# Index queries for 384 of 512 tokens, reordered layer beginnings, and chunk decays read by small DMAs

## The chip, the cores and the metric

The kernel runs on one core of a Trainium2 chip. The metric is device time in microseconds (us), the median of the runs. An execution takes 1.7 us more than its span in the profile, which runs from the first to the last instruction of the core.

## The reference

Two layers act on 512 tokens of width 1024. Each layer projects its input once and feeds two branches: an attention branch that keeps, for every query, the 128 keys with the best score of a small "indexer", and a gated linear attention (GLA) that is scanned in chunks of 64 tokens. A gated convolutional feed-forward part follows.

```python
# indexer and attention, per block of 128 queries
dots = einsum('bqhd,bsd->bqhs', q_idx, k_idx) * IDX_DIM ** -0.5
score = einsum('bqhs,bqh->bqs', relu(dots), w_idx * IDX_HEADS ** -0.5)
score = where(admissible, score, -inf)          # chunk-causal, chunks of 64
top_val, top_idx = lax.top_k(score, topk)       # topk = 128
...
# GLA, per chunk of 64
cum = cumsum(lac, axis=1); total = cum[:, -1]
k_dec = kc * exp(total[:, None] - cum)
state = exp(total)[..., None] * state + einsum('bchk,bchv->bhkv', k_dec, vc)
out = einsum('bchk,bhkv->bchv', qc, state)
```

The first 128 queries have at most 128 admissible keys, so that every one of them is kept.

## The kernel before

All projections run on TensorE as three matmuls per 128x128 block of weights (`mm3`, lines 149 to 153), since every operand is split into a high and a low half. Weights come in tiles of 512 KB by SP's queue (`pump`); ScalarE (ACT) writes the high half (line 145) and VectorE (DVE) the low half (line 146). Results of the projections are split in the same way by the same two lines. `fm_chunk` gives four banks of 128 features by 512 tokens, `tm_chunk` four banks of 128 tokens by 512 features; the next chunk uses these four banks again, so its first matmul on a bank waits for the evacuation of the one before.

A layer is a list of projections in a fixed order: index queries (iq), a small chunk (index keys, gate ranks), GLA queries (gq0 to gq3), keys (gk) and values (gv0, gv1), then queries, keys and values of the attention (aq, ak, av). In layer 0 iq comes first; in layer 1 iq is computed in two halves of 256 tokens, since the norm that ends layer 0 delivers its tokens late. Everything else is a task: a generator that `tick()` advances by one step after every six matmuls of the projections. These are the rotation tables, the index keys, the decays (`decay_task`), the loads (`load_task`), the index scores with top-k (`index_task`), the scans of GLA and then the attention. A framework turns the whole into one fixed order of instructions per engine, and gives evacuations and weight splits priority.

`staged` evacuates iq, aq and ak: bank 0 is rotated on DVE (lines 504 to 507), banks 1 to 3 are only split, and all are written to DRAM by POOL's queue (line 498) and read back per pair of heads by `load_task` (lines 525, 529, 530), since two halves of a head meet only there. `index_task` runs top-k as 16 rounds per block of 128 queries, for blocks of 512, 384 and 256 keys: a round finds the eight largest (MAX8, line 578) and takes them out (MATCH_VALUE_LOAD and MATCH_REPLACE8, line 579), each waiting for the one before.

`decay_task` multiplies the log decays with a triangle of ones (`tri`, line 449) for the suffix sums of each chunk and with two columns (`ends`, line 451) for the totals. ACT takes the exponentials; the totals are transposed (line 460) and become `dec`, which the scans multiply their state with. The evacuation of gk multiplies with the exponentials and waits for the whole task.

Of the kernel before, what the change touches and what calls it, by code (L numbers as in the profile page):

```python
# [56 lines left out]
class Trunk:  # L57
# [91 lines left out]
    def mm3(self, out, lh, ll, rh, rl, start, stop):  # L149
        mm = self.nc.tensor.matmul  # L150
        mm(out, lh, rl, start=start, stop=False)  # L151
        mm(out, ll, rh, start=False, stop=False)  # L152
        mm(out, lh, rh, start=False, stop=stop)  # L153
# [13 lines left out]
    def tm_chunk(self, l, chunk, evac):  # L167
        ps = [self.bank(self.acc) for _ in range(TB)]
        for g in range(4):
            w = self.weight((l, chunk, g)).rearrange("p z (k n) -> p z k n", k=2)  # L170
            for tb in range(TB):
                c = slice(tb * 128, (tb + 1) * 128)
                for kk in range(2):
                    k = 2 * g + kk
                    self.mm3(ps[tb], self.xT[:, k, 0, c], self.xT[:, k, 1, c], w[:, 0, kk], w[:, 1, kk],
                             k == 0, k == KT - 1)
# [5 lines left out]
    def fm_chunk(self, l, chunk, evac, toks=((0, S),), between=None, k_outer=False):  # L182

        ws = []
        ps = [self.bank(self.acc) for _ in range(4)]
        for n, (t0, t1) in enumerate(toks):
            if n:
                between()
            for g in range(4):
                if not n:  # L190
                    ws.append(self.weight((l, chunk, g)))
                w = ws[g].rearrange("p z (k n) -> p z k n", k=2)

                def mm(m, kk):
                    k, c = 2 * g + kk, slice(m * 128, (m + 1) * 128)
                    self.mm3(ps[m][:, t0:t1], w[:, 0, kk, c], w[:, 1, kk, c], self.xT[:, k, 0, t0:t1],
                             self.xT[:, k, 1, t0:t1], k == 0, k == KT - 1)
                if k_outer:
                    for m in range(4):
                        mm(m, 0)  # L200
                for m in range(4):
                    for kk in range(k_outer, 2):
                        mm(m, kk)
                    if len(toks) == 1 or m % 2:
                        self.tick()
                    if g == 3 and t1 == S:
                        with self.tc.high_priority():
                            evac(m, ps[m])
# [9 lines left out]
    def constants(self):  # L218
        nc = self.nc
        c = self.cst  # L220
        self.ident = c.tile([128, 128], F32, name="ident")
        make_identity(nc, self.ident)
        trif = self.h()
        nc.gpsimd.memset(trif[:, :128], 1.0 / 16)
        nc.gpsimd.affine_select(trif[:, :128], trif[:, :128], pattern=[[-1, 128]], base=-1, channel_multiplier=1,
                                compare_op=ALU.is_ge, fill=0.0)
        nc.gpsimd.memset(trif[64:128, 0:64], 0.0)
        nc.gpsimd.memset(trif[:, 128:262], 0.0)
        nc.gpsimd.memset(trif[0:64, 134:135], 1.0 / 16)
        nc.gpsimd.memset(trif[64:128, 135:136], 1.0 / 16)  # L230
        self.tri = c.tile([128, 128], F32R, name="tri")
        nc.vector.tensor_copy(self.tri, trif[:, :128])
        self.ends = c.tile([128, 134], F32R, name="ends")
        nc.vector.tensor_copy(self.ends, trif[:, 128:262])
# [114 lines left out]
    def plan_all(self, l):  # L349
# [4 lines left out]
        for g in range(4):  # L354
            P((l, "iq", g), (a["w_tm"][l, TM_CHUNKS.index("iq"), g], None))
        small()
        for c in self.order:
            if c.startswith("gq"):
# [32 lines left out]
    order = ["gq0", "gq1", "gk", "gv0", "gq2", "gq3", "gv1", "aq", "ak", "av"]  # L391
# [19 lines left out]
    def decay_task(self):  # L411

        nc = self.nc
# [14 lines left out]
        tot = self.bank(self.tps)  # L428
        self.expE = [self.u(F32) for _ in range(2)]

# [10 lines left out]
        for _ in range(7):  # L441
            yield
        for tb in range(TB):
            lt = ahead
            if tb < TB - 1:
                ahead = parts(tb + 1)
            e = self.bank(self.sps)
            for z in (1, 0):
                nc.tensor.matmul(e, self.tri, lt[:, z], start=z == 1, stop=z == 0)
            for z in (1, 0):  # L450
                nc.tensor.matmul(tot, self.ends[:, 6 - 2 * tb:134 - 2 * tb], lt[:, z], start=tb == 0 and z == 1,
                                 stop=tb == TB - 1 and z == 0)
            last = self.after(last, act, self.expE[tb // 2][:, tb % 2], e, AF.Exp)
            yield
            yield
        t = self.h()
        nc.scalar.copy(t[:32], tot[:32])
# [3 lines left out]
        act(self.dec, ps[:, :GH * 32].rearrange("p (h c) -> p h c", h=GH)[:, :, :8], AF.Exp)  # L461
        yield

    def ik_task(self):

        nc = self.nc
        ps = self.bank(self.tps)
# [20 lines left out]
    def staged(self, dr):  # L488
# [4 lines left out]
        rotated = []  # L493

        def write(m, src):
            t = self.u()
            self.split(t[:, 0], t[:, 1], src)
            nc.gpsimd.dma_start(rows[m], t.bitcast(F32))

        def evac(m, ps):  # L500
            if m == 0:
                self.finish(self.tables)
                x, y = self.h(), self.h()
                v.tensor_mul(x, ps, self.ropeT[:, 0])
                v.tensor_mul(y[:64], ps[64:], self.ropeT[64:, 1])
                v.tensor_mul(y[64:], ps[:64], self.ropeT[:64, 1])
                v.tensor_add(x, x, y)
                rotated.append(x)
            else:
                write(m, ps)  # L510
                if m == 1:
                    write(0, rotated[0])
        return evac

    def load_task(self, dr, dst, low=None):

        rows = dr.rearrange("(q h) n -> q h n", h=HEADS)
        load = self.nc.gpsimd.dma_start
        for _ in range(4):
            yield  # L520
        for hp in range(4):
            src = rows[:, 2 * hp:2 * hp + 2]
            t = self.u()
            if low is None:
                load(t.bitcast(F32), src)
# [312 lines left out]
    def mixer(self, l):  # L838
# [8 lines left out]
        nc.gpsimd.memset(self.gl[32:64].bitcast(F32), 0.0)  # L847
        if l == 0:
            self.tables = self.spawn(self.table_task())
            self.fm_chunk(l, "iq", self.staged(dr["iq"]), k_outer=True)  # L850
            self.do_small(l, self.sps)
        else:
            self.finish(*self.norms[:2])

            def between():
                self.finish(*self.norms)
                self.do_small(l, self.sps)
            self.fm_chunk(l, "iq", self.staged(dr["iq"]), ((0, 256), (256, 512)), between)
        iqt = self.spawn(self.load_task(dr["iq"], iqT))
        ikt = self.spawn(self.ik_task())  # L860
        dct = self.spawn(self.decay_task())
        idx = self.spawn(self.index_task(iqT, [ikt, iqt]), 1)
        self.attnT = {}
        for c in self.order:
            if c == "gk":
# [7 lines left out]
            elif c.startswith("gq"):  # L873
                h = int(c[2:])
                ps = self.fm_tile(self.weight((l, "fm", FM["gq"] + h)))
                t = self.u()
                nc.scalar.mul(t[:, 0], ps, DK ** -0.5)
                nc.vector.scalar_tensor_tensor(t[:, 1], ps, DK ** -0.5, t[:, 0].bitcast(F32), op0=ALU.mult,
                                               op1=ALU.subtract)
                self.gq[h] = t  # L880
            elif c.startswith("gv") or c == "av":
# [8 lines left out]
                self.tm_chunk(l, c, evac)  # L890
                if c != "av":
                    scans.append(self.spawn(self.scan_task(2 * int(c[2]))))
            else:
                self.fm_chunk(l, c, self.staged(dr[c]))
                self.spawn(self.load_task(dr[c], *((qT, self.ql) if c == "aq" else (kT,))))
        self.finish(*scans)
# [22 lines left out]
        self.closing(l, "wout", self.merged, 0, KT, lambda tb: self.norm_task(tb, g, b, (5, 5, 6, 11)[tb]))  # L919

# [67 lines left out]
    def ffn(self, l):  # L988
# [31 lines left out]
        self.closing(l, "wdB", gT, KA, NF, (lambda tb: self.norm_out(tb, g, b)) if l == L - 1 else lambda tb: self.norm_task(tb, g, b, (5, 5, 6, 5)[tb]))  # L1020
# [82 lines left out]
```

## Time and profile before

| | |
|---|---|
| median of 3 runs | 1770.44 us (1769.88 to 1777.11) |
| the profiled execution | 1772.71 us, span 1771.0 us |
| TensorE (PE) busy, of the span | 1746.9 us, 99% |
| weight loads (PEld) | 1429.8 us, 81% |
| VectorE (DVE) | 1129.3 us, 64% |
| ScalarE (ACT) | 717.1 us, 40% |
| GpSimd (POOL) | 70.3 us, 4% |
| DMA, mean | 111 GB/s |

PE is busy almost without a pause, so the time is the work on PE plus the few places where it waits. Matmuls overlap: a matmul of 512 columns lasts 0.39 us in a row of the profile, but the next one starts earlier, and the spacing from start to start is what it costs. The other engines matter where PE waits for them, and DVE's share of 64% is a mean over stages that differ much.

### The profile page before, as it was taken

The numbers are of one execution on the slowest core, as the hardware profiler recorded it, in microseconds if no ns is written. First come the engines' busy times: TensorE is split into PE (matmuls) and PEld (weight loads), VectorE is DVE, ScalarE is ACT, GpSimd is POOL, SyncE is SP. The second block draws the span as 40 slices with busy tenths as digits, with TensorE's granted clock in tenths as the row PEclk, the third lists the DMA queues.
The fourth block names the chain that finished last, engine by engine and source line by source line (L and its number), as shares of the span: only waits on it lengthen the run. The fifth ranks groups of instructions, "written<-read, shape, count | busy, mean of one in ns | idle before, by whom it ended". The sixth has DMA issues, their size and how long they took to land.

```text
span 1771.0 us, 21726 instructions
## 1 busy us (share of the span) xinstructions
PE 1746.9 (99%) x8312; PEld 1429.8 (81%) x8312; DVE 1129.3 (64%) x2099; ACT 717.1 (40%) x1088; POOL 70.3 (4%) x113
## 2 busy tenths in 40 slices
PE   8999999999999999999999999999999999999997
PEld 6788787888888888888787878878888888888886
DVE  6699868633476663356667997876335766633656
ACT  5644456522225442144245444664222344422430
POOL 1000300000000000000010003000000000000000
PEclk9999999999999999999999999999999999999999
DMA  7322751232423322333353229312334233222331
GB/s 239 127 76 72 213 181 60 72 107 95 167 72 108 96 96 94 95 95 97 122 177 119 72 72 267 126 48 84 107 107 166 73 107 96 95 95 94 96 107 48
DMA packets 65172, 196.65 MB, mean 111 GB/s; under 512 B 7238, under 2 KB 9542, under 8 KB 65068
## 3 DMA queue, kind: packets, MB, share of 16 engines
q1 hardware_dynamic: 51312, 152.91, 27.4%
q0 software_dynamic: 8320, 29.36, 5.3%
q10 hardware_dynamic: 5436, 12.98, 2.1%
q8 instruction: 65, 1.06, 0.2%
q14 instruction: 39, 0.32, 0.1%
HBM read 178.46 MB, written 16.78 MB: 110 GB/s over the span
## 4 chain that ended last, share of the span: by engine, by line
PE 77%; DVE 14%; DMA 3%; issue 2%; ACT 2%; POOL 1%; SPq 0%; DVEq 0%; POOLq 0%; ACTq 0%
PE ps L152 24%; PE ps L151 24%; PE ps L153 24%; DVE w L146 2%; DVE sc L579 2%; DVE m L578 1%; DVE u L146 1%; PE ps L697 1%; DVE u L800 1%; DVE h L616 1%; DMA u<-aq 1%; POOL rs L333 1%; DMA raw<-in_w_tm 1%; PE ps L707 1%; DVE xT L146 1%
## 5 line engine op out<-in xcount | busy, mean ns | idle before, releaser
L146 DVE TENSOR_TENSOR w<-raw,w 128x1024 fp32r<-128x1024 f32 (+2 forms) x287 | 349.8, 1219 | 482.4 <-ACT w L145 480.2
L151 PE MATMUL ps<-xT,w 128*128 128x512 f32 (+1 forms) x1456 | 553.7, 380 | 3.0 <-DVE xT L146 2.5
L153 PE MATMUL ps<-xT,w 128*128 128x512 f32 (+1 forms) x1456 | 551.2, 379 | 0.0
L152 PE MATMUL ps<-xT,w 128*128 128x512 f32 (+1 forms) x1456 | 550.8, 378 | 0.0
L145 ACT CAST w<-raw 128x1024 fp32r<-128x1024 f32 (+2 forms) x287 | 300.0, 1045 | 500.2 <-PE ps L153 446.4
L151 PEld LDWEIGHTS ps<-xT,w 128*128 128x128 f32 x1456 | 273.7, 188 | 56.0 <-ACT w L145 3.3
L153 PEld LDWEIGHTS ps<-xT,w 128*128 128x128 f32 x1456 | 273.5, 188 | 50.7
L152 PEld LDWEIGHTS ps<-xT,w 128*128 128x128 f32 x1456 | 273.6, 188 | 49.2 <-DVE w L146 0.2
L151 PE MATMUL ps<-w,u 128*128 128x512 f32 (+1 forms) x488 | 192.0, 393 | 0.0
L153 PE MATMUL ps<-w,u 128*128 128x512 f32 (+1 forms) x488 | 190.9, 391 | 0.0
L152 PE MATMUL ps<-w,u 128*128 128x512 f32 (+1 forms) x488 | 190.9, 391 | 0.0
L145 ACT CAST u<-h 128x512 fp32r<-128x512 f32 (+1 forms) x126 | 77.9, 619 | 219.7 <-DVE h L983 111.3
L146 DVE TENSOR_TENSOR u<-h,u 128x512 fp32r<-128x512 f32 (+1 forms) x126 | 86.3, 688 | 40.0 <-ACT u L145 39.6
L153 PEld LDWEIGHTS ps<-w,u 128*128 128x128 f32 x488 | 91.6, 188 | 21.6
L151 PEld LDWEIGHTS ps<-w,u 128*128 128x128 f32 x488 | 91.7, 188 | 21.4
L152 PEld LDWEIGHTS ps<-w,u 128*128 128x128 f32 x488 | 91.7, 188 | 20.7
L151 PE MATMUL ps<-w,xT 128*128 128x512 f32 x256 | 102.2, 399 | 0.2
L152 PE MATMUL ps<-w,xT 128*128 128x512 f32 x256 | 101.0, 395 | 0.0
L153 PE MATMUL ps<-w,xT 128*128 128x512 f32 x256 | 100.9, 395 | 0.0
L152 PE MATMUL ps<-u,w 128*128 128x512 f32 x192 | 76.0, 396 | 0.0
L151 PE MATMUL ps<-u,w 128*128 128x512 f32 x192 | 75.4, 393 | 0.0
L153 PE MATMUL ps<-u,w 128*128 128x512 f32 x192 | 74.6, 388 | 0.0
(221 smaller groups left out, 1903.4 us busy)
## 6 DMA issues: line engine op xcount, KB each, us to landing
raw<-in_w_fm SPq DMA_DIRECT2D x160, 512.0 KB, 3.6
raw<-in_w_tm SPq DMA_DIRECT2D x55, 512.0 KB, 3.6
raw<-in_w_down SPq DMA_DIRECT2D x44, 512.0 KB, 3.4
u<-aq POOLq DMA_DIRECT2D x32, 256.0 KB, 11.1
raw<-in_w_mix_out SPq DMA_DIRECT2D x16, 512.0 KB, 3.5
iq<-u POOLq DMA_DIRECT2D x8, 512.0 KB, 4.5
u<-iq POOLq DMA_DIRECT2D x8, 512.0 KB, 6.5
aq<-u POOLq DMA_DIRECT2D x8, 512.0 KB, 4.0
```

What stands on the lines that cost most here:

```text
L145: first = self.nc.scalar.copy(hi, src)
L146: self.nc.vector.tensor_sub(lo, src, hi.bitcast(F32))
L151: mm(out, lh, rl, start=start, stop=False)
L152: mm(out, ll, rh, start=False, stop=False)
L153: mm(out, lh, rh, start=False, stop=stop)
L333: self.nc.gpsimd.tensor_tensor(r, ve, self.nhalf[:, :n], ALU.pow)
L578: nc.vector.max(m8, sc)
L579: nc.vector.match_replace(sc, m8, sc, TAKEN)
L616: nc.vector.scalar_tensor_tensor(state[:, i], old[:, i], self.dec[:, h, c:c + 1], o[:, i], op0=ALU.mult, op1=ALU.add)
L697: nc.tensor.transpose(ps[:, qb * 128:(qb + 1) * 128], P[qb][:, sb * 128:(sb + 1) * 128], self.ident)
L707: mm(out[:64], v[:, :64], PT[sb][:, 1], start=False, stop=False)
L800: nc.vector.scalar_tensor_tensor(x[:, c], x[:, c], r, b[:, c], op0=ALU.mult, op1=ALU.add)
```

## The change

It does five things.

1. iq is computed, rotated, written and loaded for tokens 128 to 511 alone (`t0`, `cut`): 96 matmuls of 384 columns in each layer instead of 512. In layer 1 it is no longer in halves; the four gq tiles are (`gq_halves`).
2. The matmuls with `ends` are gone. `tri` gets its columns 63 and 127 filled, so that rows 63 and 127 of each exponential hold the total decay of a chunk. Small DMAs of POOL's queue read these rows into the tile that is transposed (line 450 of the changed kernel), and others overwrite them with ones (line 452).
3. The order becomes gv0, small, iq, gq0, gq1, gk, gq2, gq3, gv1, aq, ak, av in layer 0, and gq0 to gq3, small, iq, gk, gv0, gv1, aq, ak, av in layer 1. Tasks and scans are spawned accordingly. The first group of gv0 starts with products of high halves.
4. Bank 0 of aq is copied raw by ACT (`late`) and rotated later, in `load_task`.
5. The norm that ends layer 0 waits 11 ticks instead of 5 for its last block.

```diff
-    def mm3(self, out, lh, ll, rh, rl, start, stop):
+    def mm3(self, out, lh, ll, rh, rl, start, stop, high_first=False):
...
+    def fm_chunk(self, l, chunk, evac, t0=0):
...
+                    self.mm3(ps[m][:, t0:], w[:, 0, kk, c], w[:, 1, kk, c], self.xT[:, k, 0, t0:],
+                             self.xT[:, k, 1, t0:], k == 0, k == KT - 1)
...
+        nc.gpsimd.memset(trif[0:64, 63:64], 1.0 / 16)
+        nc.gpsimd.memset(trif[64:128, 127:128], 1.0 / 16)
...
-    order = ["gq0", "gq1", "gk", "gv0", "gq2", "gq3", "gv1", "aq", "ak", "av"]
+    order = [["gv0", "small", "iq", "gq0", "gq1", "gk", "gq2", "gq3", "gv1", "aq", "ak", "av"],
+             ["gq0", "gq1", "gq2", "gq3", "small", "iq", "gk", "gv0", "gv1", "aq", "ak", "av"]]
...
-            for z in (1, 0):
-                nc.tensor.matmul(tot, self.ends[:, 6 - 2 * tb:134 - 2 * tb], lt[:, z], start=tb == 0 and z == 1,
-                                 stop=tb == TB - 1 and z == 0)
-            last = self.after(last, act, self.expE[tb // 2][:, tb % 2], e, AF.Exp)
...
+            last = self.after(last, act, E[:, tb % 2], e, AF.Exp)
+            nc.gpsimd.dma_start(t[2 * tb:2 * tb + 2], E[63:128:64, tb % 2])
+            if tb % 2:
+                nc.gpsimd.dma_start(E[63:128:64], ones[:2])
...
-        act(self.dec, ps[:, :GH * 32].rearrange("p (h c) -> p h c", h=GH)[:, :, :8], AF.Exp)
+        nc.scalar.copy(self.dec, ps[:, :GH * 32].rearrange("p (h c) -> p h c", h=GH)[:, :, :8])
...
+            self.split(t[:, 0, cut:], t[:, 1, cut:], src[:, cut:])
+            nc.gpsimd.dma_start(rows[m][:, :, cut:], t[:, :, cut:].bitcast(F32))
...
         def evac(m, ps):
-            if m == 0:
...
+            if m == 0 and late:
+                raw = self.h()
+                nc.scalar.copy(raw, ps)
+                self.rotation = later(raw)
+            elif m == 0:
+                held.append(turn(ps))
...
+        if low is not None:
+            yield from self.rotation
...
+            if c == "small":
                 self.do_small(l, self.sps)
...
+                ikt = self.spawn(self.ik_task())
+                dct = self.spawn(self.decay_task())
+            elif c == "iq":
+                self.fm_chunk(l, c, self.staged(dr[c], cut=128), 128)
+                iqt = self.spawn(self.load_task(dr[c], iqT, cut=128))
+                idx = self.spawn(self.index_task(iqT, [ikt, iqt]))
...
+            if c == ("gk", "gv0")[l] or c == "gv1":
+                scans.append(self.spawn(self.scan_task(2 * len(scans))))
...
+    def gq_halves(self, l):
+
+        ws, pss = [], [self.bank(self.acc) for _ in range(GH)]
+        for tok in ((0, 256), (256, 512)):
+            self.finish(*self.norms[tok[0] // 128:tok[1] // 128])
+            for h in range(GH):
+                if not tok[0]:
+                    ws.append(self.weight((l, "fm", FM["gq"] + h)))
+                self.fm_tile(ws[h], tok, pss[h])
...
```

The change moves instructions on every engine. Two places are shown. The first is DVE in layer 0 at the end of ak, where DVE evacuates the four banks that av needs next. Before, in that place (h is the rotated bank 0, w a tile of weights, rs and sh belong to a scan's norm, u the splits of banks 1, 0, 2 and 3):

```order
L579 MATCH_REPLACE sc_907<-m_1971,sc_907 128x256
L581 TENSOR_SCALAR sc_907<-sc_907 128x256
L146 TENSOR_TENSOR w_2102<-raw_2100,w_2102 128x1024
L504 TENSOR_TENSOR h_2053<-ps_1830,ropeT 128x512
L505 TENSOR_TENSOR h_2054<-ps_1830,ropeT 64x512
L506 TENSOR_TENSOR h_2054<-ps_1830,ropeT 64x512
L507 TENSOR_TENSOR h_2053<-h_2053,h_2054 128x512
L146 TENSOR_TENSOR w_2135<-raw_2133,w_2135 128x1024
...
L146 TENSOR_TENSOR u_2066<-ps_1831,u_2066 128x512
L146 TENSOR_TENSOR u_2070<-h_2053,u_2070 128x512
```

Five instructions of 128x8 stand in the gap. After the change (sc_915 are the scores of the block of 384 keys, sc_1086 those of the block of 256):

```order
L502 TENSOR_TENSOR h_2017<-ps_1772,ropeT 128x512
L503 TENSOR_TENSOR h_2018<-ps_1772,ropeT 64x512
L504 TENSOR_TENSOR h_2018<-ps_1772,ropeT 64x512
L592 MAX m_1902<-sc_915 128x8
L505 TENSOR_TENSOR h_2017<-h_2017,h_2018 128x512
L593 MATCH_REPLACE sc_915<-m_1902,sc_915 128x384
L592 MAX m_1943<-sc_1086 128x8
L595 TENSOR_SCALAR sc_915<-sc_915 128x384
L593 MATCH_REPLACE sc_1086<-m_1943,sc_1086 128x256
L146 TENSOR_TENSOR w_2120<-raw_2118,w_2120 128x1024
...
L146 TENSOR_TENSOR u_2033<-ps_1773,u_2033 128x512
```

Top-k had ended ahead of the rotation before; now the last round of the block of 384 and 14 of the 16 rounds of the block of 256 stand between the rotation of bank 0 and the split of bank 1. 13 of them, from L592 MAX m_1958 to L593 MATCH_REPLACE sc_1086<-m_2140, lie where the line of dots is, with five instructions of 128x8 among them.

On PE the same place reads, after the change (ps_1772 and ps_1775 are banks 0 and 3 of ak, ps_2069 and ps_2070 banks 0 and 1 of av):

```order
L158 MATMUL ps_1772<-xT,w_1778 128x512
L156 MATMUL ps_1773<-xT,w_1778 128x512
...
L158 MATMUL ps_1775<-xT,w_1778 128x512
L156 MATMUL ps_2069<-w_1867,xT 128x512
...
L158 MATMUL ps_2069<-w_2075,xT 128x512
L156 MATMUL ps_2070<-w_1867,xT 128x512
L157 MATMUL ps_2070<-w_1867,xT 128x512
```

Between the last matmul of ak's bank 0 and the first of av's bank 1 stand 42 matmuls of 512 columns, 18 of ak and 24 of av.

The second place is POOL's queue in layer 0 (h_522 is the tile of the totals, u_520 and u_521 the exponentials, u_523 the ones, iq the stage in DRAM). Before, only writes and loads of iq stood here:

```order
L498 DMA iq_224<-u_382 128x2x512
L525 DMA u_533<-iq_224 128x1024
```

After:

```order
L450 DMA h_522<-u_520 2x512
L496 DMA iq_221<-u_612 128x2x384
...
L496 DMA iq_221<-u_616 128x2x384
L450 DMA h_522<-u_520 2x512
L450 DMA h_522<-u_521 2x512 x2
L539 DMA u_708<-iq_221 128x2x384
L452 DMA u_520<-u_523 2x1024
L452 DMA u_521<-u_523 2x1024
L539 DMA u_728<-iq_221 128x2x384
```

The transposes of the totals (line 457 after the change) wait for the four DMAs of line 450. They follow the last matmul with `tri` after 22 matmuls of 512 columns in layer 0 and 18 in layer 1.

## Rows read from the trace of the kernel before

**Rows 1.** Waits of PE: us in total, times, longest.

```profile
PE ps L469 <- ACT h L401: 3.1, 1, 3.1
...
PE ps L151 <- DVE u L146: 2.2, 3, 0.9
...
PE ps L449 <- DVE u L146: 1.5, 2, 0.8
...
PE ps L668 <- DMA u<-ak: 0.2, 1, 0.2
```

**Rows 2.** Timeline of PE: start us, us, then the instruction; 512, 384 and 256 columns.

```profile
47.03 0.39 PE L153 MATMUL ps<-xT,w 128*128 128x512 f32 x1
...
48.17 0.39 PE L152 MATMUL ps<-xT,w 128*128 128x512 f32 x1
...
83.81 0.33 PE L547 MATMUL ps<-u,u 128*128 128x384 f32 x1
83.98 0.34 PE L548 MATMUL ps<-u,u 128*128 128x384 f32 x1
84.16 0.40 PE L151 MATMUL ps<-w,xT 128*128 128x512 f32 x1
...
887.88 0.28 PE L152 MATMUL ps<-xT,w 128*128 128x256 f32 x1
888.00 0.28 PE L153 MATMUL ps<-xT,w 128*128 128x256 f32 x1
```

**Rows 3.** Groups of PE by line and form: busy us, mean ns, idle before.

```profile
L451 PE MATMUL ps<-u,ends 128*128 128x512 f32 x16 | 5.0, 392 | 0.0
```

**Rows 4.** Timeline, layer 0, around the index keys: PE, then ACT.

```profile
36.01 0.40 PE L152 MATMUL ps<-xT,w 128*128 128x512 f32 x1
39.50 0.58 PE L469 MATMUL ps<-ident,h 104*128 104x104 f32 x4 [3.10 <-ACT h L401]
...
36.43 0.62 ACT L145 CAST u<-h 128x512 fp32r<-128x512 f32 x1 [3.04 <-DVE h L507]
```

**Rows 5.** Windows: length, busy of PE, PEld, DVE, ACT, POOL, PEclk, DMA, GB/s.

```profile
40.00:43.40 3.40, 3.40 (x10) 2.65 (x10) 2.32 (x14) 1.23 (x3) 0.27 (x1) 0.51 0.95 287
...
156.00:180.00 24.00, 24.00 (x138) 19.54 (x135) 23.75 (x65) 11.47 (x19) 1.68 (x1) 1.00 0.24 69
180.00:208.00 28.00, 27.16 (x138) 22.23 (x137) 27.42 (x74) 10.78 (x16) 12.08 (x20) 1.00 0.75 213
```

**Rows 6.** Timeline of PE, layer 1: the same stage as in rows 4.

```profile
915.91 0.71 PE L422 MATMUL ps<-r,u 96*128 96x512 f32 x2
917.12 0.50 PE L151 MATMUL ps<-xT,w 128*128 128x512 f32 x1 [0.50 <-DVE u L146]
```

**Rows 7.** Timeline of DVE, layer 0: rounds of top-k, weights, rotation of ak.

```profile
195.90 0.43 DVE L578 MAX8 m<-sc 128x8 f32<-128x256 f32 x1
...
199.84 0.43 DVE L578 MAX8 m<-sc 128x8 f32<-128x256 f32 x1
200.19 1.21 DVE L146 TENSOR_TENSOR w<-raw,w 128x1024 fp32r<-128x1024 f32 x1
201.31 0.08 DVE L579 MATCH_VALUE_LOAD sc<-m,sc 128x8 f32 x1
...
207.57 0.68 DVE L504 TENSOR_TENSOR h<-ps,ropeT 128x512 f32<-128x512 f32 x1
...
208.97 0.68 DVE L506 TENSOR_TENSOR h<-ps,ropeT 64x512 f32<-64x512 f32 x1
```

**Rows 8.** Groups of ACT by form: busy us, mean ns, idle before.

```profile
L215 ACT ACTIVATE u<-ps 128x512 f32<-128x512 f32 x8 | 4.8, 598 | 6.7 <-PE ps L449 6.7
```

**Rows 9.** DMA issues: KB each, median us to landing.

```profile
ak<-u POOLq DMA_DIRECT2D x8, 512.0 KB, 8.4
...
out<-u SPq DMA_DIRECT2D x8, 128.0 KB, 1.8
...
ng<-in_norm_g ACTq DMA_DIRECT2D x2, 4.0 KB, 6.3
```

**Rows 10.** The page, part 5: weight loads of PE, mean ns.

```profile
L152 PEld LDWEIGHTS ps<-xT,w 128*128 128x128 f32 x1456 | 273.6, 188 | 49.2 <-DVE w L146 0.2
```

More of the change, by code (lines that the diff above doesn't have):

```diff
@@ L147, in split @@
         return first
-    def mm3(self, out, lh, ll, rh, rl, start, stop):
+    def mm3(self, out, lh, ll, rh, rl, start, stop, high_first=False):
         mm = self.nc.tensor.matmul
+        if high_first:
+            mm(out, lh, rh, start=start, stop=False)
+            mm(out, ll, rh, start=False, stop=False)
+            mm(out, lh, rl, start=False, stop=stop)
+            return
         mm(out, lh, rl, start=start, stop=False)
@@ L165, in fm_tile, with tm_chunk @@
         return ps
-    def tm_chunk(self, l, chunk, evac):
+    def tm_chunk(self, l, chunk, evac, k_outer=False):
         ps = [self.bank(self.acc) for _ in range(TB)]
@@ L170, in tm_chunk, with mm @@
             w = self.weight((l, chunk, g)).rearrange("p z (k n) -> p z k n", k=2)
-            for tb in range(TB):
[L172 to L176, printed above, removed]
+            def mm(tb, kk):
+                k, c = 2 * g + kk, slice(tb * 128, (tb + 1) * 128)
+                self.mm3(ps[tb], self.xT[:, k, 0, c], self.xT[:, k, 1, c], w[:, 0, kk], w[:, 1, kk],
+                         k == 0, k == KT - 1, k_outer and not g)
+            if k_outer:
+                for tb in range(TB):
+                    mm(tb, 0)
+            for tb in range(TB):
+                for kk in range(k_outer, 2):
+                    mm(tb, kk)
                 self.tick()
@@ L180, in tm_chunk @@
                         evac(tb, ps[tb])
-    def fm_chunk(self, l, chunk, evac, toks=((0, S),), between=None, k_outer=False):
-        ws = []
+    def fm_chunk(self, l, chunk, evac, t0=0):
         ps = [self.bank(self.acc) for _ in range(4)]
[L186 to L208, printed above, removed]
+        for g in range(4):
+            w = self.weight((l, chunk, g)).rearrange("p z (k n) -> p z k n", k=2)
+            for m in range(4):
+                c = slice(m * 128, (m + 1) * 128)
+                for kk in range(2):
+                    k = 2 * g + kk
+                    self.mm3(ps[m][:, t0:], w[:, 0, kk, c], w[:, 1, kk, c], self.xT[:, k, 0, t0:],
+                             self.xT[:, k, 1, t0:], k == 0, k == KT - 1)
+                self.tick()
+                if g == 3:
+                    with self.tc.high_priority():
+                        evac(m, ps[m])
     def after(self, prev, fn, *a, **k):
@@ L353, in plan_all @@
         small = lambda: P((l, "small"), (a["w_small"][l], None), KT * NSM)
[L354 to L358, printed above, removed]
+        for c in self.order[l]:
+            if c == "small":
+                small()
+            elif c.startswith("gq"):
                 fm(FM["gq"] + int(c[2:]))
@@ L427, in decay_task @@
             last = self.after(last, act, ab[i], ab[i], AF.Exp, scale=-1.0)
-        tot = self.bank(self.tps)
         self.expE = [self.u(F32) for _ in range(2)]
+        t, ones = self.h(), self.u(F32)
+        nc.gpsimd.memset(t[:32], 0.0)
+        nc.gpsimd.memset(ones[:2], 1.0)
         def parts(tb):
@@ L440, in decay_task @@
         nc.vector.tensor_sub(mn[1], mn[1], ab[1])
-        for _ in range(7):
+        for _ in range(9):
             yield
@@ L449, in decay_task @@
                 nc.tensor.matmul(e, self.tri, lt[:, z], start=z == 1, stop=z == 0)
-            for z in (1, 0):
-                nc.tensor.matmul(tot, self.ends[:, 6 - 2 * tb:134 - 2 * tb], lt[:, z], start=tb == 0 and z == 1,
-                                 stop=tb == TB - 1 and z == 0)
-            last = self.after(last, act, self.expE[tb // 2][:, tb % 2], e, AF.Exp)
+            E = self.expE[tb // 2]
+            last = self.after(last, act, E[:, tb % 2], e, AF.Exp)
+            nc.gpsimd.dma_start(t[2 * tb:2 * tb + 2], E[63:128:64, tb % 2])
+            if tb % 2:
+                nc.gpsimd.dma_start(E[63:128:64], ones[:2])
             yield
             yield
-        t = self.h()
-        nc.scalar.copy(t[:32], tot[:32])
         ps = self.bank(self.tps)
@@ L466, in ik_task @@
         nc = self.nc
+        yield
         ps = self.bank(self.tps)
@@ L486, in ik_task, with staged @@
         yield
-    def staged(self, dr):
+    def staged(self, dr, late=False, cut=0):
         nc = self.nc
@@ L492, in staged, with turn, later, load_task @@
         rows = dr.rearrange("(z m p) n -> m p z n", z=2, m=4)
-        rotated = []
+        held = []
         def write(m, src):
             t = self.u()
-            self.split(t[:, 0], t[:, 1], src)
-            nc.gpsimd.dma_start(rows[m], t.bitcast(F32))
-        def evac(m, ps):
-            if m == 0:
[L502 to L508, printed above, removed]
+            self.split(t[:, 0, cut:], t[:, 1, cut:], src[:, cut:])
+            nc.gpsimd.dma_start(rows[m][:, :, cut:], t[:, :, cut:].bitcast(F32))
+        def turn(src):
+            self.finish(self.tables)
+            x, y = self.h(), self.h()
+            c = slice(cut, S)
+            v.tensor_mul(x[:, c], src[:, c], self.ropeT[:, 0, c])
+            v.tensor_mul(y[:64, c], src[64:, c], self.ropeT[64:, 1, c])
+            v.tensor_mul(y[64:, c], src[:64, c], self.ropeT[:64, 1, c])
+            v.tensor_add(x[:, c], x[:, c], y[:, c])
+            return x
+        def later(raw):
+            x = turn(raw)
+            yield
+            write(0, x)
+            yield
+        def evac(m, ps):
+            if m == 0 and late:
[4 more added lines that the diff above has]
+                held.append(turn(ps))
             else:
                 write(m, ps)
-                if m == 1:
-                    write(0, rotated[0])
+                if m == 1 and held:
+                    write(0, held[0])
         return evac
-    def load_task(self, dr, dst, low=None):
+    def load_task(self, dr, dst, low=None, cut=0):
         rows = dr.rearrange("(q h) n -> q h n", h=HEADS)
         load = self.nc.gpsimd.dma_start
+        if low is not None:
+            yield from self.rotation
         for _ in range(4):
@@ L524, in load_task @@
             if low is None:
-                load(t.bitcast(F32), src)
+                load(t[:, :, cut:].bitcast(F32), src[:, :, cut:])
             else:
@@ L847, in mixer @@
         nc.gpsimd.memset(self.gl[32:64].bitcast(F32), 0.0)
+        idx = dct = ikt = None
         if l == 0:
             self.tables = self.spawn(self.table_task())
-            self.fm_chunk(l, "iq", self.staged(dr["iq"]), k_outer=True)
-            self.do_small(l, self.sps)
-        else:
-            self.finish(*self.norms[:2])
-            def between():
-                self.finish(*self.norms)
+        else:
+            self.gq_halves(l)
+        self.attnT = {}
+        for c in self.order[l]:
+            if c == "small":
                 self.do_small(l, self.sps)
[L858 to L865, printed above, removed]
+                ikt = self.spawn(self.ik_task())
[4 more added lines that the diff above has]
+                idx = self.spawn(self.index_task(iqT, [ikt, iqt]))
+            elif c == "gk":
                 def evac(tb, ps):
@@ L873, in mixer @@
             elif c.startswith("gq"):
[L874 to L880, printed above, removed]
+                if l == 0:
+                    h = int(c[2:])
+                    self.keep_gq(h, self.fm_tile(self.weight((l, "fm", FM["gq"] + h))))
             elif c.startswith("gv") or c == "av":
@@ L889, in evac @@
                         self.split(dst[tb][:, 0], dst[tb][:, 1], ps)
-                self.tm_chunk(l, c, evac)
-                if c != "av":
-                    scans.append(self.spawn(self.scan_task(2 * int(c[2]))))
+                self.tm_chunk(l, c, evac, k_outer=c == self.order[0][0] and l == 0)
             else:
-                self.fm_chunk(l, c, self.staged(dr[c]))
+                self.fm_chunk(l, c, self.staged(dr[c], late=c == "aq"))
                 self.spawn(self.load_task(dr[c], *((qT, self.ql) if c == "aq" else (kT,))))
+            if c == ("gk", "gv0")[l] or c == "gv1":
+                scans.append(self.spawn(self.scan_task(2 * len(scans))))
         self.finish(*scans)
@@ L919, in mixer, with keep_gq @@
         self.closing(l, "wout", self.merged, 0, KT, lambda tb: self.norm_task(tb, g, b, (5, 5, 6, 11)[tb]))
+    def keep_gq(self, h, ps):
+        t = self.u()
+        self.nc.scalar.mul(t[:, 0], ps, DK ** -0.5)
+        self.nc.vector.scalar_tensor_tensor(t[:, 1], ps, DK ** -0.5, t[:, 0].bitcast(F32), op0=ALU.mult,
+                                            op1=ALU.subtract)
+        self.gq[h] = t
+    def gq_halves(self, l):
[6 more added lines that the diff above has]
+                self.fm_tile(ws[h], tok, pss[h])
+                if tok[0]:
+                    with self.tc.high_priority():
+                        self.keep_gq(h, pss[h])
     def closing(self, l, key, src, k0, k1, norm):
```

7 lines of the change are left out of this document (1 added, 6 removed).

## The prediction, made before the changed kernel ran

> **What bounds the kernel now.** I read the waits of PE first, then PE's timeline for the price of a matmul and for the gaps, then windows and the timeline of DVE for the stage that the change rebuilds, then the list of DMAs. The waits [rows 1] are few and short; the reader is to see that next to nothing of the span is idle PE, so the kernel is bound by matmul work, and a change pays if it takes matmuls away and adds no wait. One wait is large, 3.1 us ahead of the transposes of the index keys. In the windows [rows 5] DVE is the other thing to see: from 156 to 208 us it is busy 23.75 of 24 and 27.42 of 28 us. There PE is hardly late, but DVE has no room, and DVE's fixed order decides what PE gets in time.
>
> **Matmuls taken away.** Five spacings of 512 columns take 48.17 - 47.03 = 1.14 us, 0.228 each; two of 384 columns take 84.16 - 83.81 = 0.35 us, 0.175 each [rows 2]. 192 matmuls of iq, 96 per layer, shrink from 512 to 384 columns: 192 x 0.053 = 10.2 us. That layer 1's halves of 256 columns move from iq to gq changes nothing in columns. The 16 matmuls with `ends` [rows 3] go at one spacing each: 16 x 0.228 = 3.6 us. Both lie on PE's path: **-13.8 us**.
>
> **The index keys.** In layer 0 ACT stood behind the rotation of iq's bank 0 on DVE (3.04 us) and the copy that PE wanted came late [rows 4]: 39.50 - 36.01 less one spacing is 3.3 us. Right behind it the granted clock is 0.51 for 3.4 us [rows 5], which is the 1.2 GHz level, and costs half of that, 1.7 us. Now small comes ahead of iq, so ACT has no rotation to wait for. What is late next is what layer 1 already shows in this stage, 917.12 - 915.91 less two spacings, 0.75 us [rows 6]. Net **-4.2 us**; the bounds are -5.0 and 0.
>
> **The end of iq.** The first matmul of the next chunk (gq0 in layer 0, gk in layer 1) needs iq's bank 0, 18 matmuls of 384 columns (3.2 us) after that bank was complete. DVE has to rotate it (three instructions, 2.1 us at 512 columns by 208.97 + 0.68 - 207.57 [rows 7], so 1.6 at 384 as an estimate) and stands ahead of that in the subtractions of the decays and a weight split of 1.1 us (201.31 - 200.19 [rows 7]), some 4.5 us in all. I take 1.3 us in each layer, 2.6; the wait of 1.5 us ahead of the matmuls with `tri` [rows 1] goes. Net **+1.1 us**, between -1.5 and +3.7.
>
> **The small DMAs.** No transfer of 4 KB inside the chip is in the trace. The nearest rows are 1.8 us for 128 KB to DRAM, where the queues were empty, and 6.3 us for 4 KB at the start, under heavy traffic [rows 9]. After the last matmul with `tri` the exponential takes 0.6 us [rows 8], its engine may first have a weight cast, estimated like the split at 1.1, and the matmul's own end lags by 0.16 (0.39 less a spacing): 1.9 us, then the landing d. The cover is 22 matmuls, 5.0 us, in layer 0 and 18, 4.1 us, in layer 1. PE then waits 2d - 5.3 us in both together, or only d - 2.2 in layer 1 while d is under 3.1. I take d = 3.0, since iq's writes are mostly through by the last of them: **+0.8 us**. The ends are 0 at 1.8 and 7.3 at 6.3. The Trainium skill, page "DMA: Bandwidth & Descriptors", section "Anatomy of one DMA — SWDGE (gpsimd) path", puts such a transfer at some 2.0 us fixed plus its bytes at 436 GB/s, nearly all of it completion latency, so by that page this term would be 0 and the sum 0.8 us lower; no run here shows a transfer of that size on POOL's queue. That the same rule makes four such latencies out of a result that PE had for 3.6 us of matmuls is the point at which it speaks against the change. Overwriting the rows with ones hides: gk's evacuation needs it, and PE needs that only a chunk later.
>
> **The end of ak in layer 0.** This is the largest term that the change adds. DVE executes in order. Between the rotation of ak's bank 0, which cannot begin before PE has filled that bank, and the split of bank 1, which av's bank 1 waits for, now stand a round of 384 keys and 14 of 256. Four rounds took 199.84 - 195.90 = 3.94 us, 0.985 each [rows 7], and a round waits for the one before, so nothing shortens them. From the end of bank 0: 0.16 (PE's lag) + 2.1 (three instructions of rotation) + 0.6 (the fourth) + 0.985 (the round of 384, at the least) + 0.985 + 1.1 (weights) + 13 x 0.985 = 12.8 + 0.7 (the split, as long as a rotation's instruction) = 19.4 us. PE has 42 matmuls in the meantime, 9.6 us. It waits **+9.8 us**. The bounds are 9.0, if the small instructions all fall into gaps, and 12, if DVE is late when bank 0 ends. An idle time of 3.1 us was followed by 3.4 us at the lower clock [rows 4, 5], so this one should be too: **+1.7 us**, between 0 and 2.2. The order before had all rounds ahead of the rotation. That top-k is then done costs nothing later and gives nothing back, as the softmax could begin on time before as well: its wait for ak was 0.2 us [rows 1].
>
> **Smaller terms.** In layer 1 only four rounds stand at that place, with two weight splits and the rotation: some 11 us against 40 matmuls of 512 and 12 of 256 columns, 10.6 us: +0.5 (0 to 2). DVE's full stretch has the same work under fewer matmuls; its waits were 2.2 us [rows 1], and I add 0.5 (-2.2 to +6). ak's loads stand behind one more load of aq on POOL: +0.5 (0 to 2). Bank 0 of aq copied by ACT frees the bank sooner, beside idle ACT: 0. gv0 ahead of small, and high halves first: PE starts 0.4 us sooner and waits as long for the next tile's low half: 0. The longer norm waits: 0, as layer 1's first half still needs only the first two norms.
>
> **The sum.** -13.8 - 4.2 + 1.1 + 0.8 + 9.8 + 1.7 + 0.5 + 0.5 + 0.5 = -3.1 us. The profiled execution took 1772.7 us, so 1769.6; it lies 2.3 us over the median of the runs shown, so **1767.3 us**.
>
> **The rivals.** (A) The rounds of top-k don't hold PE up and the gain stays: without 9.8 + 1.7 it is 1755.8 us. For it speaks only that I read the place from an order and not from a trace; against it, that both ends are waits between engines and the middle is one engine's own queue. It needs a round to take 0.3 us instead of 0.985. Chance 0.18. (B) Slower than before: the small DMAs land late, behind iq's writes and the weights. The place is the transposes of the totals in both layers, the price 2d - 5.3 us. It passes the gain from d = 4.6 us on. At the 8.4 us that ak's writes take [rows 9] PE waits 11.5 us, and both waits would end in the lower clock, 3.4 us more: with 0.8 taken off, 14.1 us over the forecast, 1781.4 us. Chance 0.10 of d over 4.6, some 0.06 of over 7.4. (C) Matmuls of 384 columns are no cheaper than their weight load of 188 ns [rows 10]: then iq saves 192 x 0.040 = 7.7 us and it is 1769.8. The halves of 256 columns, each with fresh weights, follow each other after 0.12 us [rows 2], so I give it 0.04. (D) The full stretch of DVE costs PE 6 us more: 1772.8, chance 0.10. The forecast itself has 0.58.
>
> **How the numbers follow.** A difference of under 0.5%, 8.9 us, can't be told from no change here. The forecast, C, D and the milder half of B lie within it. Faster by more: A and a little of the forecast's own lower edge (no lower clock, DVE better off), 0.22. Slower by more: the worse half of B and sums of upper bounds, 0.10. Same: 0.68. The range goes from just under A, 1755, to the sum of D and a mild B, 1778.
>
> **What would show it.** PE's waits should have one of 9 to 12 us in layer 0 for a split (line 146), at the second bank of av, with a row of MAX8 and MATCH_REPLACE8 of 256 keys on DVE in the same time and a window at half clock behind it. The wait of 3.1 us for line 401's copy should be gone. iq should show 0.17 to 0.18 us from start to start. The transposes of the totals should wait for line 450's DMAs under 1 us. I am wrong if that big wait is missing, if the transposes wait several microseconds, or if layer 1 shows a wait as large as layer 0's.

## The result, and the profile after

The changed kernel takes 1785.6 us (1785.11 to 1785.95), the kernel before 1775.05 us beside it: a ratio of 1.0062, with a 95% interval of 1.0049 to 1.0075. It is 0.6% slower, where 1767.3 us and "the same" were forecast, and lies over the range. The profiled execution took 1785.57 us, 12.9 us more than that of before.

The large wait that was forecast is there. From the list of PE's waits, after the change (us in total, times, longest):

```profile
PE ps L156 <- DVE u L146: 13.8, 5, 11.1
...
PE ps L156 <- DVE h L504: 1.7, 2, 0.9
...
PE ps L287 <- DVE h L283: 1.2, 1, 1.2
```

The wait of 3.1 us for line 401's copy [rows 1] is gone, and one of 11.1 us for a split has come. The timelines of PE and DVE at that place, layer 0 after the change (start us, us, instruction):

```profile
197.17 0.39 PE L158 MATMUL ps<-xT,w 128*128 128x512 f32 x1
...
206.98 0.40 PE L158 MATMUL ps<-w,xT 128*128 128x512 f32 x1
218.45 0.80 PE L156 MATMUL ps<-w,xT 128*128 128x512 f32 x1 [11.07 <-DVE u L146]
```

```profile
198.07 1.22 DVE L146 TENSOR_TENSOR w<-raw,w 128x1024 fp32r<-128x1024 f32 x1
199.20 0.69 DVE L502 TENSOR_TENSOR h<-ps,ropeT 128x512 f32<-128x512 f32 x1
...
205.04 0.42 DVE L592 MAX8 m<-sc 128x8 f32<-128x256 f32 x1
...
216.84 0.43 DVE L592 MAX8 m<-sc 128x8 f32<-128x256 f32 x1
...
217.71 0.68 DVE L146 TENSOR_TENSOR u<-ps,u 128x512 fp32r<-128x512 f32 x1
```

PE ends ak's bank 0 with the matmul of 197.17, the rotation begins at 199.20, the 13 rounds of 256 keys run from 205.04 to 217.7 us at 0.98 us each, as before [rows 7], and the split that PE waits for ends at 218.39. Nothing on DVE is slow; it is the order. The windows at the same place, and one in the feed-forward part of layer 0, which the change does not touch:

```profile
207.40:218.40 11.00, 0.00 (x0) 0.00 (x0) 10.45 (x40) 6.11 (x12) 0.00 (x0) 0.74 0.84 199
218.40:222.80 4.40, 4.35 (x10) 3.51 (x11) 3.82 (x10) 0.00 (x0) 3.65 (x6) 0.50 0.60 223
...
600.00:800.00 200.00, 200.00 (x859) 160.94 (x858) 93.95 (x109) 66.48 (x80) 0.00 (x0) 1.00 0.30 95
```

The same last window of the kernel before:

```profile
600.00:800.00 200.00, 200.00 (x869) 162.90 (x868) 95.85 (x111) 67.26 (x81) 0.00 (x0) 1.00 0.30 95
```

The first two rows show PE empty for 11 us and then 4.4 us at a granted clock of 0.50, the 1.2 GHz level. The other two show what the prediction had not looked for. PE is busy all 200 us at full clock in both, in the same stage of the same work, yet does 859 matmuls where it did 869: 200/859 = 0.2328 us from start to start instead of 0.2301. A matmul loads one tile into the engine and streams the other past it; a row names the streamed tile first, so `ps<-xT,w` streams xT past loaded weights and `ps<-w,u` streams weights past a loaded u. Over the matmuls of 512 columns that stream xT past weights, some 3,350 that follow one of their kind, the mean spacing is 0.2334 us, and was 0.2292 before: 14.0 us. Those that stream weights past u, the second largest kind, stayed at 0.2333.

So there are two costs to explain: 11.1 us of wait with its lower clock, and 14 us of pace.

### The profile page after: what moved, and what is told of

Same layout as the page of the kernel before. It is cut to its first block, busy times and chain, and to the rows that moved or that the text cites. A ratio compares the mean times of both kernels' runs of the same rounds, so it can differ in the third digit from the quotient of the medians.

```text
span 1783.8 us, 21734 instructions
## 1 busy us (share of the span) xinstructions
PE 1749.3 (98%) x8296; PEld 1426.9 (80%) x8296; DVE 1127.0 (63%) x2098; ACT 715.5 (40%) x1088; POOL 81.5 (5%) x128
## 4 chain that ended last, share of the span: by engine, by line
PE 84%; DVE 9%; issue 2%; DMA 2%; ACT 1%; POOL 1%; SPq 0%; DVEq 0%; ACTq 0%; POOLq 0%
PE ps L156 26%; PE ps L157 26%; PE ps L158 26%; DVE w L146 1%; DMA u<-aq 1%; PE ps L711 1%; POOL rs L328 1%; DVE u L146 1%; DVE u L814 1%; PE ps L721 1%; DVE sc L593 1%; PE ps L682 1%; PE ps L683 1%; PE ps L618 1%; PE ps L562 0%
## 5 line engine op out<-in xcount | busy, mean ns | idle before, releaser
L156 PE MATMUL ps<-xT,w 128*128 128x512 f32 (+3 forms) x1456 | 555.1, 381 | 3.9 <-DVE xT L146 2.0
L158 PE MATMUL ps<-xT,w 128*128 128x512 f32 (+3 forms) x1456 | 551.3, 379 | 0.0
L157 PE MATMUL ps<-xT,w 128*128 128x512 f32 (+3 forms) x1456 | 550.8, 378 | 0.0
L156 PEld LDWEIGHTS ps<-xT,w 128*128 128x128 f32 (+1 forms) x1456 | 273.6, 188 | 57.6 <-ACT w L145 3.2
L158 PEld LDWEIGHTS ps<-xT,w 128*128 128x128 f32 (+1 forms) x1456 | 273.2, 188 | 53.9
L157 PEld LDWEIGHTS ps<-xT,w 128*128 128x128 f32 (+1 forms) x1456 | 273.4, 188 | 50.1
L145 ACT CAST u<-h 128x512 fp32r<-128x512 f32 (+2 forms) x126 | 77.7, 618 | 200.3 <-DVE h L1011 111.4
L156 PE MATMUL ps<-w,xT 128*128 128x512 f32 x248 | 99.9, 403 | 12.8 <-DVE u L146 11.4
L146 DVE TENSOR_TENSOR u<-h,u 128x512 fp32r<-128x512 f32 (+2 forms) x126 | 86.1, 687 | 39.2 <-ACT u L145 38.9
L157 PE MATMUL ps<-w,xT 128*128 128x512 f32 x248 | 99.1, 400 | 0.0
L158 PE MATMUL ps<-w,xT 128*128 128x512 f32 x248 | 98.9, 399 | 0.0
```

Of the source, the lines that this page charges most:

```text
L145: first = self.nc.scalar.copy(hi, src)
L146: self.nc.vector.tensor_sub(lo, src, hi.bitcast(F32))
```

## The experiments

**The theory for the pace** is place in memory. `ends` was a tile of 536 bytes per partition among the constants, and took 544. Without it every tile behind, the large buffers u and the weights too, lies 544 bytes lower; xT, the first tile, has not moved. In the program's layout the weights lay 171,456 bytes above xT before, 64 below a multiple of 512, and now 96 below one. The rivals: the new order of the work, or the chip. **The theory for the wait** is the order of the rounds; its rival, that DVE is full and the wait would come back elsewhere.

**1. 32 bytes more ahead of all tiles but xT, changed kernel.**

```diff
+        self.pad = c.tile([128, 8], F32, name="pad")
+        nc.gpsimd.memset(self.pad, 0.0)
         self.nhalf = c.tile([128, 16], F32, name="nhalf")
```

> The changed kernel with one unused tile of 32 bytes per partition among the constants, so that every tile behind it lies 32 bytes higher and starts at a multiple of 64 bytes again, as in the kernel before; no instruction moves but one memset. Theory (place in memory): the matmuls that stream xT past weights (3,500 of 512 columns) go from 0.2335 us from start to start back to 0.2294, 14 us less: 1771 to 1773 us where the changed kernel takes 1785.6; the wait of 11.1 us in layer 0 stays. Rival (the new order of the work or a slower day of the chip makes the pace): no change, 1784 to 1787 us.

1773.99 us, ratio 0.9994 (0.9982 to 1.0006): 11.6 us less for 32 unused bytes. The spacing is 0.2302 us, not quite the 0.2294 expected, and the wait stays at 11.2 us.

**2. The same edit in the kernel before.**

> The kernel before with the same unused tile of 32 bytes, so that its tiles now start 32 bytes past a multiple of 64. Theory (place in memory): the spacing of the matmuls that stream xT past weights rises from 0.2294 to about 0.2335 us, and the time by 12 to 16 us over the kernel before. Rival (order of the work): no change beyond 3 us.

1783.55 us, ratio 1.0055 (1.0036 to 1.0074), spacing 0.2332 us. In the window of the feed-forward part:

```profile
600.00:800.00 200.00, 200.00 (x858) 160.45 (x858) 94.67 (x109) 65.88 (x79) 0.00 (x0) 1.00 0.29 93
```

The kernel before, with its old order, does 858 matmuls in 200 us. The rival falls: no order of work and no other day of the chip is needed for the slow pace.

**3. aq's bank 0 rotated at once, changed kernel.**

```diff
-                self.fm_chunk(l, c, self.staged(dr[c], late=c == "aq"))
+                self.fm_chunk(l, c, self.staged(dr[c]))
...
-        if low is not None:
-            yield from self.rotation
```

> The changed kernel with aq's bank 0 rotated at its evacuation, as before, instead of late; the rest of the change stays. In DVE's order the 14 rounds of top-k no longer stand between the rotation and the splits of ak. Theory (those rounds hold PE up): the wait of 11.1 us goes down to 1 to 2 us and the lower clock behind it goes (2.2 us): 1772 to 1775 us. Rival (DVE is simply full there, and the wait comes back at another place): PE's waits in layer 0 between 150 and 240 us still sum to over 10 us, 1783 to 1786 us.

1774.82 us, ratio 1.0006 (0.9995 to 1.0016). PE at av's second bank, then DVE around the split of bank 1:

```profile
208.86 0.51 PE L156 MATMUL ps<-w,xT 128*128 128x512 f32 x1 [1.37 <-DVE u L146]
```

```profile
207.79 0.43 DVE L590 MAX8 m<-sc 128x8 f32<-128x256 f32 x1
208.14 0.67 DVE L146 TENSOR_TENSOR u<-ps,u 128x512 fp32r<-128x512 f32 x1
...
211.03 0.43 DVE L590 MAX8 m<-sc 128x8 f32<-128x256 f32 x1
```

1.37 us are left of 11.07. The rounds have not moved ahead of the rotation, which begins at 199.39 here and at 199.20 in the changed kernel. Of the 16 rounds of 256 keys, four begin between the rotation and the split of bank 1, and the other twelve now follow the splits, from 211.03 to 224.9 us, where PE has no wait. DVE is busy 86.90 of the 90 us from 150 to 240, more than the 76.84 of the changed kernel, yet PE's waits there sum to 2.7 us, with 12.4 in the changed kernel. So the rival falls: it is the order and not the amount of work. The granted clock stays at 1.00 behind the wait, and the pace stays slow (859 matmuls in the window of the feed-forward part).

**4. Both edits.**

> Both edits together: the changed kernel with 32 bytes more among the constants and aq rotated at once. If the two causes are separate the gains add: 1758 to 1761 us, 0.7% to 0.9% faster than the kernel before, since the work that the change takes off PE (13.8 us) then shows. If they share a cause: not below the better of the two alone.

1762.61 us, ratio 0.9930 (0.9908 to 0.9951), where the gains of the two, 11.6 and 10.8 us, add up to 1763.2 us. The causes are separate, though the time lies 1.6 us over the range expected, as experiment 1 gave back less than the 14 us of the pace.

**5. The 32 bytes ahead of the weights alone, changed kernel.**

```diff
+        self.gap = pool("gap", 1)
         self.wsp = pool("wsp", 5)
...
+        self.pad = self.gap.tile([128, 8], F32, name="pad")
```

> The changed kernel with the unused 32 bytes right ahead of the pool of split weights, so that only the weights start at a multiple of 64 bytes again; all other tiles stay 32 bytes past one. Theory (the place of the weights sets the pace): spacing of the matmuls that stream xT past weights 0.2295 to 0.2302 us as with all tiles shifted, 1771 to 1775 us. Rival (it is the place of the other tiles, or of all together): 0.2333 us, 1784 to 1787 us.

1774.19 us, ratio 1.0000 (0.9990 to 1.0011), spacing 0.2293 us. The place of the weights is enough.

**6. The 32 bytes ahead of xT too, kernel before.**

```diff
+        self.pad = self.cst.tile([128, 8], F32, name="pad")
         self.xT = self.cst.tile([128, KT, 2, S], F32R, name="xT")
```

> The kernel before with the unused 32 bytes ahead of xT, so that xT and all tiles behind it start 32 bytes past a multiple of 64 and keep their distances. Theory (each operand's own place counts): 0.2331 us or slower, 1783 to 1788 us. Rival (the distance of weights and xT counts): 0.2292 us and the time of the kernel before, 1770 to 1776 us.

1772.99 us, ratio 0.9998 (0.9981 to 1.0014), spacing 0.2292 us. The theory as I had put it falls, and the rival holds: with xT and all tiles behind it moved by 32 bytes the pace is the old one, and with all but xT moved (experiment 2) it is slow. What counts is the distance between the two operands.

**7. 64 bytes in place of 32, kernel before.**

> The kernel before with 64 unused bytes ahead of the same tiles as with 32 bytes, so that they start at another multiple of 64. Theory (multiples of 64 bytes): spacing 0.2292 us and the time of the kernel before within 2 us. Rival (multiples of 128 or more, or any shift): slower by over 5 us.

1771.01 us, ratio 0.9976 (0.9959 to 0.9993), spacing 0.2277 us: neither theory nor rival. The pace is faster than before, with the weights now at a multiple of 512 bytes from xT.

**8. aq rotated at once and 96 bytes, changed kernel.** The weights again lie a multiple of 512 bytes from xT.

> The changed kernel with aq rotated at once and 96 unused bytes instead of 32: weights at a multiple of 128 bytes, where the kernel before had them 64 past one. Theory (multiples of 64 bytes alone): the same as with 32 bytes, 1761 to 1764 us. Rival (a wider grid): a spacing below 0.2290 us and 1750 to 1758 us, or above 0.2300 and over 1766 us.

1754.92 us, ratio 0.9892 (0.9875 to 0.9910), spacing 0.2277 us. Here the rival, a wider grid, holds.

**9. Two distances, changed kernel, and 10. kernel before.** The edits of 1 and 5 together with other sizes: 9 has 160 bytes among the constants and 64 ahead of the weights, with aq rotated at once; 10 has only the 64 bytes.

> The changed kernel with aq rotated at once, 160 unused bytes among the constants and 64 ahead of the weights: weights and the large buffers u both lie a multiple of 128 bytes from xT, and so from each other (weights at 128 past a multiple of 512 from xT; with 96 bytes it was a multiple of 512). Theory (distance of the two operands modulo 128, for every pair): matmuls that stream u past weights, 0.2333 us in every run so far with a distance of 64, come down to about 0.2280 as well, 1,464 x 0.005 = 8 us: 1746 to 1749 us. Rival (only xT counts): 0.2333 stays, 1753 to 1757 us. Rival (multiples of 512 count): xT's matmuls rise over 0.2290, 1758 us or more.

> The kernel before with 64 unused bytes ahead of the weights: weights and u a multiple of 512 bytes from xT and from each other, no other edit. Theory (distance modulo 128): xT's matmuls 0.2277 us (3,590 x 0.0015 = 5 us) and u's 0.2280 (8 us), 1759 to 1763 us where the kernel before takes about 1774. Rival (only xT counts): 1768 to 1771 us.

9 took 1764.35 us, ratio 0.9948 (0.9933 to 0.9963): the matmuls of weights and u came down to 0.2271 us, as the theory had it, but xT's rose to 0.2330, as the rival of multiples of 512 had it. (The expectation has these operands the wrong way round: what it calls u streamed past weights, 1,464 matmuls, are the rows `ps<-w,u`, weights streamed past u.) A multiple of 128 bytes is not enough. 10 took 1758.66 us, ratio 0.9914 (0.9898 to 0.9931), with 0.2275 and 0.2270. Of the distances tried only multiples of 512 are the fastest.

**11. Both distances a multiple of 512, aq rotated at once, and 12. the same with aq rotated late,** the change as it is but for its place in memory.

> The changed kernel with aq rotated at once, 32 unused bytes among the constants and 64 ahead of the weights, so that weights and u both lie a multiple of 512 bytes from xT and from each other. In all runs so far a pair of operands streamed at 0.2270 to 0.2290 us where the weights lie a multiple of 512 bytes from the streamed tile, at 0.229 to 0.230 where they lie 64 less, and at 0.2326 to 0.234 at 32, 64, 96, 128, 384, 416 or 480. Theory (the distance modulo 512): xT's matmuls 0.2277, u's 0.2271, so 8 us less than the 1754.9 of the run with 96 bytes: 1743 to 1748 us, the fastest so far. Rival (another grid, met by chance): a pair over 0.2300, over 1752 us.

> The changed kernel as it is, aq's rotation late, with the same two unused tiles, so that it differs from the run before it by the late rotation alone. Theory: the wait of 11 us in layer 0 and the lower clock behind it (2.2 us) cost 11 to 14 us over the run with the rotation at once: 1756 to 1760 us; the change as a whole then is level with the kernel before at the same distances (1758.7), as the prediction had it. Rival (the wait was made worse by the slow matmuls): under 8 us more.

11 took 1745.06 us, ratio 0.9834 (0.9818 to 0.9851), and is the fastest kernel. 12 took 1756.05 us, ratio 0.9896 (0.9882 to 0.9911): 11.0 us for the late rotation alone, at the lower edge of the 11 to 14 expected, and close to the 10.8 us at the slow pace (experiment 3). The feed-forward window of 12:

```profile
600.00:800.00 200.00, 200.00 (x884) 165.48 (x883) 98.84 (x114) 68.23 (x82) 0.00 (x0) 1.00 0.31 95
```

The next table has, for the two largest kinds of matmul, the place of the loaded tile less that of the streamed one, in bytes modulo 512 (from the layout that the program is built with), the mean spacing in us from start to start of matmuls of 512 columns (worked out from the traces), and the count of matmuls in the window of the feed-forward part, 600 to 800 us:

| kernel | xT past weights | spacing | weights past u | spacing | in the window |
|---|---|---|---|---|---|
| before, and 6 | 448 | 0.2292 | 64 | 0.2333 | 869, 869 |
| after, and 3 | 416 | 0.2334 | 64 | 0.2333 | 859, 859 |
| 1 and 4 | 448 | 0.2302, 0.2297 | 64 | 0.2333 | 865, 864 |
| 2 | 480 | 0.2332 | 64 | 0.2333 | 858 |
| 5 | 448 | 0.2293 | 32 | 0.2333 | 869 |
| 7 and 8 | 0 | 0.2277 | 64 | 0.2333 | 875, 874 |
| 9 | 128 | 0.2330 | 0 | 0.2271 | 868 |
| 10, 11, 12 | 0 | 0.2275 | 0 | 0.2270 | 884, 883, 884 |

The two smaller kinds fit. Weights streamed past xT take 0.2333 us in the kernel before (distance 64), 0.2340 in the changed one (96), 0.2325 in 9 (384) and 0.2285 to 0.2291 in 7, 8 and 10 to 12 (0). u streamed past weights takes 0.2290 to 0.2296 us at 448, 0.2330 in 5 (480) and 0.2271 to 0.2275 in 9 to 12 (0).

## Why the prediction was wrong

The failing step is the one that priced the matmuls: it took the spacing of 0.228 us as given for all matmuls that stay, and counted only those that go. Removing `ends` was booked as 3.6 us of matmuls saved, and as nothing else. It also moved the weights by 544 bytes against xT, and that cost 14.0 us over work that the change doesn't touch. No rival had it. The profiled execution was forecast at 1769.6 us and took 1785.57, 16.0 us more: 14.0 are the pace, and 1.8 are the end of ak in layer 0 (below); the other misses are smaller and go both ways. At equal distances the sum comes out near: experiment 12 against experiment 10, the change as it is against the kernel before, is 1756.05 - 1758.66 = -2.6 us, and -3.1 were forecast. That it is so near is partly luck: the terms below miss to both sides, and the profiled execution of experiment 10 waited 2.4 us for ak's loads in layer 0, where the kernel before did not.

Point by point, for the rest:

- **Matmuls taken away.** iq's spacing is as priced. Ten in a row, the first and the last:

```profile
44.69 0.34 PE L158 MATMUL ps<-xT,w 128*128 128x384 f32 x1
...
46.28 0.34 PE L158 MATMUL ps<-xT,w 128*128 128x384 f32 x1
```

  1.59/9 = 0.177 us, with 0.175 forecast. Rival C is out.
- **The index keys.** The wait went and so did the lower clock behind it. But its size was that of one execution: in experiment 6, whose order is that of before, PE waited 1.35 us there and the clock stayed at 1.00, in experiment 10 it waited 3.7 us and the clock fell to 0.50. And the transposes of the rotation tables, nearer to the start now, wait 1.2 us (line 287), where 0.75 had been put for what is late next. So this part saved 3.1 + 1.7 - 1.2 = 3.6 us against the profiled execution of before, 0.1 against experiment 6 and 4.2 against experiment 10; the 4.2 of the forecast is the upper end.
- **The end of iq.** Two waits of 0.87 us for the rotation (line 504, 1.7 us in all), where 2.6 were forecast; with the wait ahead of the matmuls with `tri` gone that is +0.2 and not +1.1.
- **The small DMAs.** Their median to landing is 3.7 us, with 3.0 forecast. The list of DMA issues, after:

```profile
h<-u POOLq DMA_DIRECT2D x8, 4.0 KB, 3.7
```

  But PE waits for the last of the four in a layer, and that one is quicker: the six others, issued around iq's four writes, took 3.2 to 4.6 us, the last one 2.2 us in layer 0 and 1.6 in layer 1. The landings of line 450, layer 0 from 65.8 to 66.2 us, then layer 1 from 957.2 to 958:

```profile
DMA to landing us min/median/max: 2.2/2.2/2.2
```

```profile
DMA to landing us min/median/max: 1.6/1.6/1.6
```

  So PE did not wait, in layer 1 either, where the cover is shorter. The last of the four there, on POOL, and the transposes on PE:

```profile
957.39 0.54 POOL L450 DMA_DIRECT2D h<-u  x1 [2.24 <-ACT u L213]
```

```profile
959.80 0.39 PE L156 MATMUL ps<-w,xT 128*128 128x512 f32 x1
960.12 0.43 PE L457 MATMUL ps<-ident,h 32*128 32x32 f32 x4
```

  The transposes follow 0.32 us after the matmul ahead of them, in layer 0 as well (69.23 to 69.55). The reason given, that iq's writes are mostly through by then, held, the 3.0 us put for d were too long, and the term is 0 and not +0.8. With the median of 3.7 us PE would have waited in layer 1. Rival B is out. The Trainium skill, page "DMA: Bandwidth & Descriptors", section "Anatomy of one DMA — SWDGE (gpsimd) path", has 2.0 us; the two transfers that decide, 2.2 and 1.6 us, lie near it, and the six others do not.
- **The end of ak.** 11.1 us with 9.8 forecast. From the rotation to the end of the split DVE took 218.39 - 199.20 = 19.2 us, with 19.3 forecast (19.4 less PE's lag). What was missing is that DVE began late: bank 0's last matmul ended at 197.56, and a round of 384 keys and a split of weights held the rotation up until 199.20. That was the reason given for the upper bound of 12. The lower clock lasted 4.4 us of PE's work, 2.2 us, with 1.7 forecast. Rival A, that the rounds don't hold PE up, is out: with the order of experiment 3 the wait is 1.37 us.
- **The full stretch of DVE.** PE's waits for splits apart from the large one are 13.8 - 11.1 = 2.7 us, with 2.2 before and 0.5 more forecast. Rival D is out.

## What to carry to other kernels

Before a difference is put down to the edit, compare the spacing of a stage that the edit doesn't touch: a window with the count of matmuls shows a change of pace at once. Taking a constant away moves every tile behind it, so the distances of the operands that PE reads belong to the layout that is chosen. And where PE waits for an instruction that another engine can only reach behind others, add up what stands between that engine's own release and that instruction; here that sum came within 0.1 us of the trace, and only the engine's late start was missing.

## What the runs showed of the hardware

Matmuls of 512 columns with a fresh load for each follow each other after 0.227 us where the loaded tile lies a multiple of 512 bytes from the streamed one (0.229 for weights streamed past xT), 0.229 to 0.230 where it lies 448 past one, and 0.2325 to 0.234 at 32, 64, 96, 128, 384, 416 and 480: up to 2.8% on a kernel that is bound by them, and 29.5 us between the changed kernel and experiment 12. Moving both operands by 32 bytes had no effect (experiment 6). Odd and even multiples of 512 are equally fast (335 x 512 bytes from xT to the weights in 7 and 10, 334 x 512 in 8, 11 and 12), so the grid is not wider than 512; a distance of 256 was not tried. The Trainium skill, page "SBUF — State Buffer", section "Operand start alignment", asks only that a tile starts at a multiple of its element and says that its runs timed nothing, so it neither agrees nor disagrees. Why the distance counts stays open. So does the spread at 448: experiments 1 and 4, with one and the same layout, have 0.2302 and 0.2297 us, and experiment 5, with u not moved, 0.2293.

Transfers of 4 KB from one place of the memory on the core to another, on POOL's queue, landed after 1.6 and 2.2 us as the last of a group, and after 3.2 to 4.6 us around four writes of 384 KB.
